# Sums of squares and first-part scaling in the last part of a hybrid attention trunk, rearranged over VectorE, TensorE and GpSimd

## The chip, the cores and the metric

The kernel runs on one core of one Trainium2 chip, in float32 (products are split into a rounded high part and a low part, three matmuls for each). The metric is the device time of one execution in microseconds, given as the median of several runs.

## The reference

One layer of a decoder trunk over 1,024 tokens of width 2,048: two groups of attention heads, an output projection, a gated embedding, and a last normalisation. What the change touches is the end:

```python
gate = jax.nn.sigmoid(rmsnorm(h, norm_ple_g[i]) @ w_ple_gate[i])
h = h + gate * (p[i] @ w_ple_proj[i])
return rmsnorm(h, norm_final_g)

def rmsnorm(x, g, eps=NORM_EPS):
    xf = x.astype(jnp.float32)
    y = xf * lax.rsqrt(jnp.mean(xf * xf, axis=-1, keepdims=True) + eps)
    return (y * g.astype(jnp.float32)).astype(x.dtype)
```

The last `rmsnorm` needs, for each token, the sum of squares over all 2,048 features before any feature of that token can be scaled and written.

## The kernel before

Features lie on the partitions: the 2,048 are 16 chunks of 128, and tokens run along the free axis. The 1,024 tokens are two halves of 512. The last stage finishes the second of them to be done, half 0. Chunks u and u + 8 are worked as a pair u = 0 to 7, held in `hpair[u]`, [128, 2, 512], with c = 0 or 1 for the member of the pair. For each pair TensorE makes two gate products, called S3 and A22, into one PSUM bank; VectorE adds and multiplies, ScalarE applies the sigmoid, VectorE adds gate times embedding to h, and the squares of h are added up in the tile `s2`.

Pairs 0 to 5 run in a loop over the whole half. Pairs 6 and 7 are written out by hand, in two quarters of 256 tokens: `TQ[0]` (the first part) and `TQ[1]` (the last quarter). The steps, each for a pair u, a member c and a quarter tq:

- `partly(u, nm, tq)`: the 24 matmuls (8 chunks, three each, L2055 to L2057) of one gate product on one quarter; it can call a function between its two halves of 12.
- `begun`: two VectorE operations, L2062 (adds the PSUM bank) and L2063 (times the root that the gate's normalisation needs).
- `sigm`: sigmoid on ScalarE, L2067.
- `ended`: two VectorE operations, L2072 (times the embedding, in PSUM) and L2073 (adds to h).
- `squared`: the square on ScalarE, L2081; for the very last one, pair 7, c = 0, last quarter, on VectorE, L2079.
- `gained`: ScalarE multiplies h by the last normalisation's weight, L2086.
- `mean`: matmuls with a constant matrix of 1/128 sum `s2` and the four squares of pairs 6 and 7 over the partitions, for the first part (L2091, L2093). `root` makes the inverse root from it (L97 to L101).
- `finals(u)`: VectorE multiplies pair u of the first part by the root, [128, 2, 256], L1955, and SyncE issues its transfer to the output, L1956.
- `mean_t`: the sums for the last quarter, with tokens on the partitions: each matmul takes 128 tokens of squares as weights and one column of the constant (L2100, L2102); `j` is which 128 tokens. `root_t` makes the root (L2116 to L2121).
- `turned`: TensorE transposes the last quarter's blocks (L2134) so that `leave` can multiply by the root, one value for each partition, on ScalarE (L2143) or VectorE (L2145) and send them (L2148, L2151): eight blocks of 256 KB.
- `late.popleft()()`: products of the other half that wait to be written, L1963 on VectorE.

TensorE, VectorE and ScalarE execute this in the order written. GpSimd's and SyncE's instructions are put in order by a planner that plays the program through with its own costs; each queue then executes in that fixed order, so a transfer that waits for its data holds what is queued behind it.

## Time and profile before

| | before |
|---|---|
| median of 3 runs | 2390.8 us (2389.43 to 2391.39) |
| profiled execution, its own time | 2393.36 us |
| its span | 2391.5 us |
| TensorE matmul busy | 2360.9 us (99%) |
| VectorE busy | 1864.1 us (78%) |
| ScalarE busy | 1201.7 us (50%) |
| GpSimd busy | 238.6 us (10%) |
| granted TensorE clock, mean | 0.998 |

The profile is of one execution; times in it are microseconds from the start of its span. PE is TensorE, DVE VectorE, ACT ScalarE, POOL GpSimd, SPq the queue from which SyncE issues transfers. A timeline row has the start, the duration, the engine, the line, what is written and read, and how many instructions were merged into it; a bracket tells how long the engine had been idle and what released it. Rows of matmuls overlap, so their pace is the distance between starts. A row of the view by windows has the stretch, its length, the busy time of PE, PE weight loads, DVE, ACT and POOL with their counts, then the granted clock, the DMA engines' share and GB/s.

### The profile page before, as it was taken

What the parts mean: (1) busy time and instruction counts of PE and PEld (TensorE: products, weight loads), DVE (VectorE), ACT (ScalarE), POOL (GpSimd) and SP (SyncE); (2) the same over time, 40 slices, a digit from 0 to 9 for tenths busy, and PEclk for the clock granted to TensorE, in tenths of its full rate; (3) what the DMA queues carried; (4) which work ended last, traced back from release to release, by engine and by line L of the source; (5) the groups of instructions that cost most, each with busy time, mean ns of one, the idle gap of its engine ahead of it and who ended that gap; (6) DMA issues with size and microseconds to landing.
All of it is one profiled execution on the core that took longest, in us unless ns stands there. A gap on an engine that the chain in (4) does not pass through costs nothing.

```text
span 2391.5 us, 32647 instructions
## 1 busy us (share of the span) xinstructions
PE 2360.9 (99%) x11318; PEld 1969.1 (82%) x11318; DVE 1864.1 (78%) x3245; ACT 1201.7 (50%) x2163; POOL 238.6 (10%) x367
## 2 busy tenths in 40 slices
PE   9999999999999999999999999999999999999998
PEld 7787878888888888888888888888788888778877
DVE  7888777777877778788888876766887987677787
ACT  6243345555556445555555556545642435532455
POOL 1211110000000000000000000110121121011000
PEclk9999999999999999999999999999999999999999
DMA  8787765444456777434444455666798889898965
GB/s 266 264 284 231 233 209 156 149 156 135 125 148 215 257 251 255 127 107 114 117 122 126 112 158 187 202 200 214 215 234 192 267 245 278 291 342 294 320 206 183
DMA packets 219413, 489.53 MB, mean 205 GB/s; under 512 B 24688, under 2 KB 36208, under 8 KB 219248
## 3 DMA queue, kind: packets, MB, share of 16 engines
q1 hardware_dynamic: 159728, 347.43, 44.3%
q0 software_dynamic: 42960, 109.86, 18.0%
q10 hardware_dynamic: 16560, 30.15, 3.7%
q8 instruction: 89, 1.46, 0.2%
q14 instruction: 76, 0.62, 0.1%
HBM read 336.09 MB, written 159.65 MB: 207 GB/s over the span
## 4 chain that ended last, share of the span: by engine, by line
PE 80%; issue 7%; DMA 5%; DVE 4%; ACT 3%; POOL 1%; SPq 0%; ACTq 0%; POOLq 0%; DVEq 0%
PE acc L240 14%; PE acc L242 14%; PE acc L241 14%; PE tp L415 2%; PE pbc L630 2%; PE pbc L628 2%; PE pbc L629 2%; PE z L319 1%; PE z L318 1%; PE pa L630 1%; PE pa L628 1%; PE pb L1733 1%; PE pb L1734 1%; PE pb L1735 1%; PE pa L629 1%
## 5 line engine op out<-in xcount | busy, mean ns | idle before, releaser
L240 PE MATMUL acc<-xh,whi 128*128 128x512 f32 x1152 | 464.6, 403 | 0.0
L242 PE MATMUL acc<-xh,wlo 128*128 128x512 f32 x1152 | 450.8, 391 | 0.1
L241 PE MATMUL acc<-xl,whi 128*128 128x512 f32 x1152 | 450.3, 391 | 0.0
L162 ACT CAST whi<-wraw 128x1024 fp32r<-128x1024 f32 x192 | 201.7, 1050 | 123.4 <-PE acc L241 109.5
L242 PEld LDWEIGHTS acc<-xh,wlo 128*128 128x128 f32 x1152 | 216.2, 188 | 48.2 <-DVE wlo L157 0.5
L721 ACT CAST wpr<-T 128x512 fp32r<-128x512 f32 x144 | 87.8, 620 | 325.3 <-DVE T L680 228.4
L241 PEld LDWEIGHTS acc<-xl,whi 128*128 128x128 f32 x1152 | 217.2, 189 | 37.7 <-issue 0.2
L240 PEld LDWEIGHTS acc<-xh,whi 128*128 128x128 f32 x1152 | 216.8, 188 | 38.1 <-issue 0.2
L157 DVE TENSOR_TENSOR wlo<-wraw,whi 128x1024 fp32r<-128x1024 f32 x160 | 195.4, 1221 | 45.2 <-ACT whi L162 43.2
L434 ACT CAST awh<-tp 128x256 fp32r<-128x256 f32 (+1 forms) x160 | 80.6, 504 | 167.4 <-PE tp L415 166.8
L370 ACT ACTIVATE et<-z,mx 128x512 f32<-128x512 f32 (+7 forms) x128 | 94.7, 740 | 61.7 <-DVE mx L364 53.3
L439 DVE TENSOR_TENSOR awl<-tp,awh 128x256 fp32r<-128x256 f32 (+1 forms) x160 | 92.4, 578 | 41.7 <-ACT awh L434 41.5
L721 ACT CAST wpr<-wraw 128x512 fp32r<-128x512 f32 x112 | 68.6, 615 | 105.3 <-DMA wraw<-tw_d 38.1
L349 DVE TENSOR_TENSOR_SCAN st<-pt 128x511 f32<-128x511 f32 (+3 forms) x64 | 86.7, 1355 | 22.3 <-ACT pt L342 20.7
L735 DVE TENSOR_TENSOR wpr<-T,wpr 128x512 fp32r<-128x512 f32 x144 | 98.6, 685 | 3.6 <-ACT wpr L721 2.3
L364 DVE TENSOR_REDUCE mx<-z 128x1 f32<-128x512 f32 (+7 forms) x128 | 97.0, 758 | 4.4
L735 DVE TENSOR_TENSOR wpr<-wraw,wpr 128x512 fp32r<-128x512 f32 x112 | 76.0, 685 | 20.2 <-ACT wpr L721 20.2
L240 PE MATMUL acc<-cA12h,whi 128*128 128x512 f32 x192 | 75.9, 395 | 0.0
L240 PE MATMUL acc<-cA11h,whi 128*128 128x512 f32 x192 | 75.6, 394 | 0.0
L342 ACT ACTIVATE pt<-z 128x512 f32<-128x512 f32 (+3 forms) x64 | 41.6, 650 | 67.0 <-DVE z L326 63.1
L241 PE MATMUL acc<-cA12l,whi 128*128 128x512 f32 x192 | 75.2, 392 | 0.0
L242 PE MATMUL acc<-cA12h,wlo 128*128 128x512 f32 x192 | 75.1, 391 | 0.0
(580 smaller groups left out, 6206.9 us busy)
## 6 DMA issues: line engine op xcount, KB each, us to landing
wraw<-w_in SPq DMA_DIRECT2D x192, 512.0 KB, 3.7
wraw<-w_gate SPq DMA_DIRECT2D x92, 256.0 KB, 5.9
wraw<-w_out SPq DMA_DIRECT2D x72, 256.0 KB, 4.5
wraw<-w_vg SPq DMA_DIRECT2D x71, 256.0 KB, 4.3
wlo_d<-wlo SPq DMA_DIRECT2D x32, 512.0 KB, 3.6
wlo<-wlo_d SPq DMA_DIRECT2D x32, 512.0 KB, 4.3
h_d<-hc POOLq DMA_DIRECT2D x56, 256.0 KB, 4.9
comb_d<-sg POOLq DMA_DIRECT2D x48, 256.0 KB, 7.4
```

What stands on the lines that cost most here:

```text
L157: V.tensor_tensor(lo[:, o], raw[:, o], hi[:, o].bitcast(F32), op=ALU.subtract)
L162: side.later(1, lambda: A.copy(hi[:, o], raw[:, o]))
L240: T.matmul(acc[c], hi[:, k2, kh, c, :], xh, start=first, stop=False)
L241: T.matmul(acc[c], hi[:, k2, kh, c, :], xl, start=False, stop=False)
L242: T.matmul(acc[c], lo[:, k2, kh, c, :], xh, start=False, stop=last)
L349: V.tensor_tensor_scan(st[:, off + 1:nkey], pt[:, off:nkey - 1], pt[:, off:nkey - 1], initial=1.0, op0=ALU.mult, op1=ALU.bypass)
L364: V.reduce_max(mx, z[:, vw], axis=AX.X, negate=True)
L370: A.activation(et[:, vw], z[:, vw], AF.Exp, bias=mx[:, 0:1], accum_out=l)
L434: A.copy(wh[:, o, :], tp[:, o, :])
L439: V.tensor_tensor(wl[:, o, :], tp[:, o, :], wh[:, o, :].bitcast(F32), op=ALU.subtract)
L721: A.copy(t[:, 0], src)
L735: V.tensor_tensor(t[:, 1], src, t[:, 0].bitcast(F32), op=ALU.subtract)
```

## The change

For the first part, the squares of three of the four blocks of pairs 6 and 7 are added into `s2` by VectorE (`fold`), so that `mean` has two matmuls where it had five; and `mean` is called between the two halves of the second S3 product of the last quarter, where it stood ahead of that product. For the last quarter, the sums of pairs 6 and 7 (c = 1), which stood in the middle of the last gate product, are made behind it, after the first transposes, in one PSUM tile of two columns where there were two tiles; `root_t` handles the two columns in one operation. The transposes into `ps` stand behind the last sums. Pairs 2 to 5 of the first part are multiplied by GpSimd (`eng=G`), and pairs 6 and 7 by VectorE at earlier places.

```diff
-        def final(r, u):
+        def final(r, u, eng=V):
             t = hpair[u][:, :, TQ[0]]
-            V.tensor_tensor(t, t, r.unsqueeze(1).to_broadcast([P, 2, Q]), op=ALU.mult)
+            eng.tensor_tensor(t, t, r.unsqueeze(1).to_broadcast([P, 2, Q]), op=ALU.mult)
...
-        def mean(*es):
+        def fold(u, c):
+
+            V.tensor_tensor(s2[:, TQ[0]], s2[:, TQ[0]], sqs.pop((u, c, 0)), op=ALU.add)
+
+        def mean():
 
             ms[0] = pp.tile([P, Q], F32, name="ssps", tag="t")
             T.matmul(ms[0], ones, s2[:, TQ[0]], start=True, stop=False)
-            for e in es:
-                T.matmul(ms[0], ones, sqs.pop(e + (0,)), start=False, stop=e == (7, 0))
+            T.matmul(ms[0], ones, sqs.pop((7, 0, 0)), start=False, stop=True)
 
         def mean_t(*es):
 
+            new = 1 not in ms
+            if new:
+                ms[1] = pp.tile([P, 2], F32, name="ssps", tag="t")
             for j in range(2):
-                if (1, j) not in ms:
-                    ms[1, j] = pp.tile([P, 1], F32, name="ssps", tag="t")
-                    T.matmul(ms[1, j], s2[:, Q + j * P:Q + j * P + P], ones[:, 0:1], start=True, stop=False)
+                o, js = ms[1][:, j:j + 1], slice(j * P, j * P + P)
+                if new:
+                    T.matmul(o, s2[:, TQ[1]][:, js], ones[:, 0:1], start=j == 0, stop=False, skip_group_check=True)
                 for e in es:
-                    T.matmul(ms[1, j], sqs[e + (1,)][:, j * P:j * P + P], ones[:, 0:1], start=False, stop=e == (7, 0))
+                    T.matmul(o, sqs[e + (1,)][:, js], ones[:, 0:1], start=False, stop=e == (7, 0) and j == 1, skip_group_check=True)
...
         def root_t():
-            for j in range(2):
-                A.activation(rq[:, j:j + 1], ms[1, j], AF.Ln, bias=eps6[:, 0:1], scale=1.0 / NK)
+            A.activation(rq, ms[1], AF.Ln, bias=eps6[:, 0:1], scale=1.0 / NK)
             A.activation(rq, rq, AF.Exp, scale=-0.5)
-            for j in range(2):
-                V.scalar_tensor_tensor(rn[:, j:j + 1], ms[1, j], EPS * NK, rq[:, j:j + 1], op0=ALU.add, op1=ALU.mult)
+            V.scalar_tensor_tensor(rn, ms[1], EPS * NK, rq, op0=ALU.add, op1=ALU.mult)
...
         begun(6, 0, 0)
+        fold(6, 1)
         squared(7, 1, 0)
...
         begun(7, 0, 0)
+        fold(7, 1)
         squared(6, 0, 0)
...
         tables(LOGS)
+        fold(6, 0)
         late.popleft()()
         begun(6, 1, 1)
-        mean((6, 1), (7, 1), (6, 0), (7, 0))
-        partly(7, "S3", 1)
+        partly(7, "S3", 1, mean)
         root()
         tables(SIGS)
         finals(0)
+        finals(2, 3, 4, 5, eng=G)
         begun(7, 1, 1)
...
-        partly(7, "A22", 1, lambda: mean_t((6, 1), (7, 1)))
-        finals(2, 3, 4)
+        partly(7, "A22", 1)
         ended(6, 0, 1)
...
-        finals(5)
+        finals(6)
         zA = pz.tile([P, 2, HALF], F32, name="oz", tag="z")
         ps = [pp.tile([P, HALF], F32, name="oa", tag="acc", bufs=2) for _ in range(2)]
         for j in range(2):
             turned(zA[:, j, :], 0, j)
-        turned(ps[0], 1, 0)
-        mean_t((6, 0))
-        turned(ps[1], 1, 1)
+        mean_t((6, 1), (7, 1), (6, 0))
         ended(7, 0, 1)
         squared(7, 0, 1)
         gained(7, 0, 1)
-        finals(6)
+        finals(7)
         mean_t((7, 0))
+        for j in range(2):
+            turned(ps[j], 1, j)
...
         leave(zA[:, 1, :], 0, 1, A)
-        finals(7)
         leave(zB[:, 0, :], 2, 0, A)
```

More of the change, by code (lines that the diff above doesn't have):

```diff
@@ L2114, in root_t, with finals @@
         def root_t():
-            for j in range(2):
-                A.activation(rq[:, j:j + 1], ms[1, j], AF.Ln, bias=eps6[:, 0:1], scale=1.0 / NK)
+            A.activation(rq, ms[1], AF.Ln, bias=eps6[:, 0:1], scale=1.0 / NK)
             A.activation(rq, rq, AF.Exp, scale=-0.5)
-            for j in range(2):
-                V.scalar_tensor_tensor(rn[:, j:j + 1], ms[1, j], EPS * NK, rq[:, j:j + 1], op0=ALU.add, op1=ALU.mult)
+            V.scalar_tensor_tensor(rn, ms[1], EPS * NK, rq, op0=ALU.add, op1=ALU.mult)
             V.scalar_tensor_tensor(rn, rn, -0.5 / NK, rq, op0=ALU.mult, op1=ALU.mult)
             V.scalar_tensor_tensor(rq, rn, 1.5, rq, op0=ALU.add, op1=ALU.mult)
-        def finals(*us):
+        def finals(*us, eng=V):
             for u in us:
-                final(r0, u)
+                final(r0, u, eng)
         BLOCKS = [[(u, 0) for u in range(4)], [(u, 1) for u in range(4)],
```

## The prediction

> **What bounds the kernel now.** I read the page first, then the timelines of TensorE, VectorE, ScalarE and SyncE over the last 40 us, then the busy time by windows of the last ten.

> ```profile
> span 2391.5 us, 32647 instructions
> PE 80%; issue 7%; DMA 5%; DVE 4%; ACT 3%; POOL 1%; SPq 0%; ACTq 0%; POOLq 0%; DVEq 0%
> ```

> The chain that ended last is TensorE for 80% of the span, so until the last product of the last quarter every TensorE instruction taken out is worth its pace. The change touches only what is issued after about 2354 us. These are TensorE's rows there that matter (start, duration; duration overlaps, so the pace is read from the starts):

> ```profile
> 2364.65 0.59 PE L2091 MATMUL ssps<-s,onesr 128*128 128x256 f32 x2
> 2365.08 1.89 PE L2093 MATMUL ssps<-sq,onesr 128*128 128x256 f32 x8
> 2366.62 0.47 PE L2055 MATMUL pbq<-cgS3h,wpr 128*128 128x256 f32 x1
> 2366.93 0.28 PE L2056 MATMUL pbq<-cgS3l,wpr 128*128 128x256 f32 x1
> 2367.05 0.28 PE L2057 MATMUL pbq<-cgS3h,wpr 128*128 128x256 f32 x1
> ...
> 2374.00 0.28 PE L2100 MATMUL ssps<-onesr,s 128*128 128x1 f32 x2
> ...
> 2375.26 0.36 PE L2055 MATMUL pbq<-cgA22h,wpr 128*128 128x256 f32 x1
> 2375.46 0.28 PE L2056 MATMUL pbq<-cgA22l,wpr 128*128 128x256 f32 x1
> ...
> 2376.77 1.04 PE L2134 MATMUL oz<-ident,h 128*128 128x128 f32 x8
> ...
> 2379.77 0.61 PE L2102 MATMUL ssps<-onesr,sq 128*128 128x1 f32 x4 [0.68 <-DVE sq L2079]
> ```

> TensorE runs without a gap to the last product, which ends at 2376.77. From there VectorE, ScalarE and the transfers set the end: TensorE itself then waits 0.68 us for the last square. VectorE's rows:

> ```profile
> 2360.97 0.42 DVE L2072 TENSOR_TENSOR qt<-qt,ple 128x256 f32<-128x256 f32 x1 [0.48 <-ACT qt L2067]
> ...
> 2363.80 0.42 DVE L2072 TENSOR_TENSOR qt<-qt,ple 128x256 f32<-128x256 f32 x1 [0.48 <-ACT qt L2067]
> ...
> 2367.97 0.42 DVE L99 SCALAR_TENSOR_TENSOR r<-ssps,r 128x256 f32<-128x256 f32 x1 [1.83 <-ACT r L98]
> ...
> 2369.34 0.69 DVE L1955 TENSOR_TENSOR h<-h,r 128x512 f32<-128x512 f32 x1
> 2369.95 0.42 DVE L2062 TENSOR_TENSOR qt<-pbq,qt 128x256 f32<-128x256 f32 x1
> 2370.41 0.42 DVE L2063 TENSOR_TENSOR qt<-qt,sums 128x256 f32<-128x256 f32 x1
> ...
> 2373.39 0.42 DVE L2063 TENSOR_TENSOR qt<-qt,sums 128x256 f32<-128x256 f32 x1
> 2373.73 1.89 DVE L1955 TENSOR_TENSOR h<-h,r 128x512 f32<-128x512 f32 x3
> 2375.53 0.41 DVE L2072 TENSOR_TENSOR qt<-qt,ple 128x256 f32<-128x256 f32 x1
> ...
> 2376.97 0.42 DVE L2062 TENSOR_TENSOR qt<-pbq,qt 128x256 f32<-128x256 f32 x1 [0.56 <-PE pbq L2057]
> 2377.43 0.43 DVE L2063 TENSOR_TENSOR qt<-qt,sums 128x256 f32<-128x256 f32 x1
> 2377.78 0.68 DVE L1955 TENSOR_TENSOR h<-h,r 128x512 f32<-128x512 f32 x1
> 2378.38 0.41 DVE L2072 TENSOR_TENSOR qt<-qt,ple 128x256 f32<-128x256 f32 x1
> ...
> 2379.29 0.42 DVE L2079 TENSOR_TENSOR sq<-h 128x256 f32<-128x256 f32 x1
> ...
> 2381.39 0.16 DVE L2121 SCALAR_TENSOR_TENSOR r<-r,r 128x2 f32<-128x2 f32 x1
> ```

> Here VectorE has no gap from 2367.97 to 2376.4, so it is nearly as full as TensorE. The root of the last quarter is ready at 2381.55, and only then can the eight output blocks leave. How they leave:

> ```profile
> 2382.30 1.31 SPq L2148 DMA_DIRECT2D out_dram<-hc  x3
> 2383.71 0.41 SPq L1956 DMA_DIRECT2D out_dram<-h  x1
> 2384.21 0.62 SPq L2151 DMA_DIRECT2D out_dram<-hc  x1
> ```
> ```profile
> 2384.00:2385.00 1.00, 0.00 (x0) 0.00 (x0) 0.00 (x0) 1.00 (x3) 0.00 (x0) 1.00 1.05 385
> 2388.00:2389.00 1.00, 0.00 (x0) 0.00 (x0) 0.00 (x0) 0.00 (x0) 0.00 (x0) 0.50 1.04 342
> ```

> The two columns at the end are the DMA share and GB/s: all 16 engines are full, at about 345 GB/s, to the end. Eight blocks of the last quarter and one of the first part (the row at L1956 that stands between them) drain here, 9 x 262,144 B, some 6.8 us.

> **The change, part by part.** *Sums of the first part.* Five products of squares become two. The five run from 2364.65 to 2366.62: 1.97 us, 0.394 each. Three fewer take 1.18 us from TensorE; the two that stay still switch between the two kinds of product once, as now (the 0.31 from 2366.62 to 2366.93 in place of the pace of 0.12 from 2366.93 to 2367.05). They also move behind twelve products, 12 x 0.12 = 1.44 us, so the sum itself comes 1.44 - 1.18 = 0.26 us later, and with it VectorE's steps from 2367.97 on.

> *The three folds* are VectorE operations of 128x256, 0.42 us each. The first two fall where VectorE now waits 0.48 us for a sigmoid, the third in the 1.83 us before L99: nothing. The cover is thin for the first two; what ran over would come out of the same 1.83 us. TensorE's new wait, for the third fold, is at about 2366.1, and the fold ends by about 2365.1; queued behind it are twelve products, so a late fold would cost TensorE directly, but it has 1 us in hand.

> *The last quarter's sums* leave the middle of the last product: 2374.00 to 2375.26, 1.26 us, and the slower restart (0.20 to 2375.46 in place of 0.12), 1.34 us in all. The last product then ends at 2376.77 - 1.18 - 1.34 = 2374.25, and VectorE's 0.56 us of waiting for it at 2376.97 goes. The moved sums stand where TensorE waits for the last square anyway.

> *Four blocks to GpSimd.* VectorE loses three in the row at 2373.73 (to 2375.53, 1.80 us) and one at 2377.78 (to 2378.38, 0.60 us); one that came after the square, block 6, now lies before it (0.60). What is late next is ScalarE: with nothing between, a sigmoid separates L2063 from L2072 by 0.91 us (0.43 running, 0.48 waiting as in the row at 2360.97). So the last stretch is, from the L2063 of block (6,0), now at 2373.39: +0.26 for the late root, +0.91 to its L2072 at 2374.56, +0.46 and +0.35 (the pitches from 2376.97 to 2377.43 and 2377.78, which the pair L2072, L2073 shares) to the next L2062 at 2375.37, the same to block 6 at 2376.18, +0.60 to the last L2072 at 2376.78, +0.91 to the square (2378.38 to 2379.29 now) at 2377.69. That is 1.60 us before 2379.29.

> *The root of the last quarter* does two operations on ScalarE and VectorE as one each:

> ```profile
> 2378.33 1.28 ACT L2105 ACT_TABLE_LOAD   x1
> 2379.62 0.51 ACT L2086 ACTIVATE qt<-h,gvec 128x256 f32<-128x256 f32 x1
> 2380.19 0.48 ACT L2116 ACTIVATE r<-ssps,eps 128x1 f32<-128x1 f32 x2
> ```

> Half of 0.48 is 0.24, and VectorE's pair gives 0.07 more. The root is then ready 1.60 + 0.31 = 1.91 us earlier, at 2379.6. The table load and the gain hang on the last sigmoid, which moves by the same 1.60, so they end as closely before the sums as now.

> *The leaving blocks.* They start 1.91 us earlier. Block 7 of the first part, now fourth in this queue, is finished by 2378.7 and has drained before the first block leaves: one of nine transfers, 262,144 B at 345 GB/s, 0.76 us (0.50 if SyncE's issue sets the pace: 2383.71 to 2384.21). I take 0.66. The transposes that move behind the last sums are done by the time their copies ask for them.

> The sum is -1.91 - 0.66 = **-2.6 us**: a span of 2388.9, and a run of 2393.36 - 2.6 = 2390.8 for the profiled one. That run lay 2.56 above the median of the runs shown, 2390.8; against the median the forecast is **2388.2**.

> **What GpSimd's operations cost.** No arithmetic of GpSimd is in the trace. The nearest rows:

> ```profile
> 973.20 0.96 POOL L1394 MEMSET qz<- 128x1024 f32 x1 [9.04 <-PE tp L415]
> ```
> ```profile
> 973.77 0.69 DVE L1427 TENSOR_TENSOR qk<-qk,sw 128x512 f32<-128x512 f32 x1
> ```

> GpSimd writes 1,024 elements in 0.96 us, 512 in 0.48: one pass over a block. A product reads two and writes one, so it costs 0.48 to 1.44 us; I take 1.2, near three passes. Four of them, from 2369.6, end at 2374.4, behind them SyncE issues their transfers in its own order, then blocks 1, 6, 7. The leaving blocks come at 2380.4 (2382.30 less 1.91); up to 2369.6 + 4p + 4 x 0.76 = 2380.4, p = 1.9 us each, the four are covered, and at 2.6 each (4 x 0.65 = 2.6 us later) their transfers would have eaten up the gain. [...]

> A second unknown is what it does to VectorE. In these rows a VectorE product of two SBUF tensors takes its usual 0.69 us while the memset runs, so the lower bound is nothing, and I take nothing. The upper bound is that they take turns, the first rival.

> **The rivals.** *Turns.* If a GpSimd product and a VectorE operation with two SBUF operands exclude each other, GpSimd gets in whenever VectorE runs L2062 or L2072, whose one operand is in PSUM. It then holds the next operation, L2063 or L2073, for 1.2 less the 0.46 between them (2369.95 to 2370.41): 0.74 us, four times, 3.0 us. All of it lands on the chain above, which is VectorE's: -2.6 + 3.0 = +0.4, 2391.2 (2390.4 at 1.0 us a product, 2392.1 at 1.44). For it: VectorE is full from 2369 on, and seven of its operations there have two SBUF operands. Against it: the memset's row, which reads nothing and so tests only half. [...]

> *Turns with a long product.* If GpSimd's first products are slower than three passes, as code it has not run before here, the same mechanism ends on the other side. At (2.6 + 4.8) / 4 + 0.46 = 2.3 us each the kernel is 4.8 us (0.2%) slower; at 2.5 us it is 8.2 - 2.6 = +5.6, 2396.4. Against it: 2.3 us would be nearly five passes.

> *More gain.* With VectorE never in the way, the last square still needs the last product at 2374.25 and the chain behind it: from 2376.77 to 2379.29 now, less the 0.60 of L1955 in it, 1.9 us. That is at most 1.5 us better than forecast, 2386.7, still within 0.2%.

> **How the numbers follow.** Side by side 0.52, turns 0.36, turns with a long product 0.12. About 0.2%, 4.8 us, is what a measurement of this kernel can tell from no change. The first two lie within it; I give 0.06 of the first to faster, for runs that scatter (2389.43 to 2391.39 before) and terms read too small, and 0.11 of the last to slower. So 0.06, 0.83, 0.11. The range goes from the most gain, 2386.7, less 0.7 of scatter, 2386.0, to turns at 1.44 us a product, 2392.1, with 1.4 of scatter, 2393.5; it leaves the long product out.

> **What would show it.** Right: two products of squares in the middle of the second S3 product and L2055 to L2057 without a gap otherwise; the last product ending near 2374.3; four GpSimd rows of about 1.2 us; VectorE's L2063 and L2073 beside them at 0.42; the last square about 1.6 us earlier; no L1956 transfer among the leaving blocks. Turns would show as L2063, L2073 or L1955 rows lengthened to over 1 us, or gaps before them, each ending with a GpSimd row. Wrong altogether: GpSimd rows over 2 us, SyncE holding finished blocks behind them, or a TensorE gap before the moved sums.

## The result: 0.15% slower, and the profile after

The median went from 2390.7 us (15 runs, 2388.09 to 2393.65) to 2395.6 us (15 runs, 2391.28 to 2398.08): a ratio of 1.0015, 95% interval 1.0008 to 1.0022, or 1.9 to 5.3 us slower. The forecast was 2388.2, with 2386.0 to 2393.5 as its range; the measured median lies above it.

The profiled execution after the change has a span of 2390.8 us (2392.68 us its own time), less than the 2391.5 before. That isn't the change: whole executions scatter by some us ahead of the part that it touches. So everything below is read in the *tail*: from the end of pair 6's S3 product on the last quarter (with the change, the start of pair 7's) to the end of the span. Before, that is 2364.65 to 2391.5, 26.85 us; with the change, 2361.20 to 2390.8, **29.60 us**, 2.75 longer. A later profile of each gave 26.86 and 29.66, with starts at 2361.94 and 2364.64: the tail repeats to 0.1 us, its start doesn't repeat to 3.

VectorE's timeline with the change, from the first part's root on (columns as before):

```profile
2366.65 0.42 DVE L2062 TENSOR_TENSOR qt<-pbq,qt 128x256 f32<-128x256 f32 x1
2367.10 1.06 DVE L2063 TENSOR_TENSOR qt<-qt,sums 128x256 f32<-128x256 f32 x1
2368.08 1.78 DVE L1955 TENSOR_TENSOR h<-h,r 128x512 f32<-128x512 f32 x1
2369.79 0.41 DVE L2072 TENSOR_TENSOR qt<-qt,ple 128x256 f32<-128x256 f32 x1
2370.23 1.07 DVE L2073 TENSOR_TENSOR h<-h,qt 128x256 f32<-128x256 f32 x1
2371.22 0.41 DVE L2072 TENSOR_TENSOR qt<-qt,ple 128x256 f32<-128x256 f32 x1
2371.66 1.04 DVE L2073 TENSOR_TENSOR h<-h,qt 128x256 f32<-128x256 f32 x1
...
2377.08 0.42 DVE L2079 TENSOR_TENSOR sq<-h 128x256 f32<-128x256 f32 x1
...
2380.69 0.16 DVE L2125 SCALAR_TENSOR_TENSOR r<-r,r 128x2 f32<-128x2 f32 x1
```

L2063 and L2073 took 0.42 or 0.43 before, L1955 0.69. Four of them are longer here by 0.64, 1.09, 0.64 and 0.62: 2.99 us. L2062 and L2072, which take one operand from PSUM, are as before. There is no gap: the waiting is inside the row, counted as busy. GpSimd's timeline, one row at a time:

```profile
2366.24 1.64 POOL L1955 TENSOR_TENSOR h<-h,r 128x512 f32<-128x512 f32 x1 [89.96 <-DVE r L101]
```
```profile
2367.84 1.47 POOL L1955 TENSOR_TENSOR h<-h,r 128x512 f32<-128x512 f32 x1
```
```profile
2369.27 1.74 POOL L1955 TENSOR_TENSOR h<-h,r 128x512 f32<-128x512 f32 x1
```

Each lengthened VectorE row ends 0.3 us (L1955 0.6 us) after one of these: VectorE's operation seems to begin when GpSimd's is over. The fourth starts at 2370.97 and takes 1.45. Now TensorE:

```profile
2362.64 0.59 PE L2095 MATMUL ssps<-s,onesr 128*128 128x256 f32 x2
2363.07 0.59 PE L2096 MATMUL ssps<-sq,onesr 128*128 128x256 f32 x2
2363.32 0.47 PE L2055 MATMUL pbq<-cgS,wpr 128*128 128x256 f32 x1
...
2370.58 0.28 PE L2057 MATMUL pbq<-cgA22h,wpr 128*128 128x256 f32 x1
2374.50 1.18 PE L2138 MATMUL oz<-ident,h 128*128 128x128 f32 x8 [3.64 <-issue]
2375.48 0.42 PE L2106 MATMUL ssps<-onesr,s 128*128 128x1 f32 x2
...
2377.47 2.27 PE L2108 MATMUL ssps<-onesr,sq 128*128 128x1 f32 x10
2379.60 1.95 PE L2138 MATMUL oa<-ident,h 128*128 128x128 f32 x8
2381.34 1.92 PE L2138 MATMUL oz<-ident,h 128*128 128x128 f32 x8
```

The last product is early, as forecast. Then TensorE stands for 3.64 us. The bracket names no releaser; in the kernel's text the first transposes reuse the PSUM space that block (6,0) reads last in its L2072, and that L2072, late on VectorE, ends at 2374.40, 0.1 us before they start. The transposes from 2379.60 then go at 0.22 us each (1.74 us for eight); before, eight took 0.93 us (2380.23 to 2381.16). The view by windows shows why; the third column from the end is the granted clock:

```profile
2374.50:2375.00 0.50, 0.50 (x5) 0.50 (x6) 0.50 (x2) 0.11 (x1) 0.00 (x0) 1.00 0.00 0
2375.00:2375.50 0.50, 0.50 (x7) 0.50 (x5) 0.47 (x2) 0.50 (x2) 0.00 (x0) 0.81 0.00 0
2375.50:2376.00 0.50, 0.50 (x5) 0.50 (x4) 0.50 (x2) 0.50 (x2) 0.00 (x0) 0.50 0.00 0
...
2385.50:2386.00 0.50, 0.00 (x0) 0.00 (x0) 0.00 (x0) 0.21 (x1) 0.00 (x0) 0.95 1.04 348
```

Less than a microsecond after TensorE has taken up work again, its clock falls to one half, and it stays there for 10.2 us, to the end of its work. Before, it fell at 2385.5, 3.2 us after the last transpose, where it cost nothing. The last quarter's sums, which were to be done as the last square comes, are now late:

```profile
2379.78 0.26 ACT L2121 ACTIVATE r<-ssps,eps 128x2 f32<-128x2 f32 x1 [1.85 <-PE ssps L2108]
```

and the blocks leave with a hole, since the fourth waits for transposes (ScalarE's copy for it starts at 2383.29, after a wait of 1.14 us for them): SyncE's timeline has no block of the first part among them, as forecast, but the fourth issue starts 1.1 us after the third has ended.

```profile
2381.60 1.31 SPq L2152 DMA_DIRECT2D out_dram<-hc  x3
2384.00 0.62 SPq L2155 DMA_DIRECT2D out_dram<-hc  x1
```

### The profile page after: what moved, and what is told of

It is laid out like the page before. It is cut to its first block, busy times and chain, and to the rows that moved or that the text cites. A ratio compares the mean times of both kernels' runs of the same rounds, so it can differ in the third digit from the quotient of the medians.

```text
span 2390.8 us, 32644 instructions
## 1 busy us (share of the span) xinstructions
PE 2361.9 (99%) x11312; PEld 1971.8 (82%) x11312; DVE 1865.2 (78%) x3243; ACT 1202.2 (50%) x2162; POOL 244.9 (10%) x371
## 4 chain that ended last, share of the span: by engine, by line
PE 75%; issue 11%; DVE 5%; DMA 4%; ACT 3%; POOL 2%; ACTq 0%; POOLq 0%; SPq 0%; DVEq 0%
PE acc L240 14%; PE acc L242 14%; PE acc L241 14%; PE tp L415 2%; PE pbc L630 2%; PE pbc L628 2%; PE pbc L629 2%; PE z L319 1%; PE z L318 1%; PE av L462 1%; DMA wraw<-w_gate 1%; PE av L461 1%; PE av L460 1%; PE pb L1733 1%; PE pb L1734 1%
```

## The experiments

Every kernel's tail, cut at the end of the last square (L2079) and at the last step of the last quarter's root, in us, all from the profiled executions:

| kernel | tail starts | to last square | to root | to the end | tail |
|---|---|---|---|---|---|
| before | 2364.65 | 15.06 | 1.84 | 9.95 | 26.85 |
| before, again | 2361.94 | 15.05 | 1.85 | 9.96 | 26.86 |
| the change | 2361.20 | 16.30 | 3.35 | 9.95 | 29.60 |
| the change, again | 2364.64 | 16.32 | 3.37 | 9.97 | 29.66 |
| before + GpSimd | 2367.36 | 17.24 | 2.53 | 9.97 | 29.74 |
| change without GpSimd | 2359.53 | 15.16 | 2.27 | 9.94 | 27.37 |
| change, TensorE kept busy | 2363.23 | 16.35 | 1.78 | 9.34 | 27.47 |
| without GpSimd, kept busy | 2359.66 | 15.14 | 1.79 | 9.61 | 26.54 |
| the same, pair 6 moved | 2361.72 | 14.55 | 2.03 | 9.10 | 25.68 |
| before + first part's sums | 2363.34 | 14.54 | 1.85 | 9.97 | 26.36 |
| before + last quarter's sums | 2366.68 | 14.40 | 1.95 | 9.97 | 26.32 |
| best of these parts | 2361.91 | 14.55 | 1.79 | 9.15 | 25.49 |

Theory at this point: GpSimd and VectorE take turns (3.0 us), and the pause that this leaves on TensorE halves its clock (some 2.5 us). Rival: one of the two is only a by-product.

**GpSimd alone.** On the kernel before:

```diff
         finals(0)
+        finals(2, 3, 4, 5, eng=G)
...
-        finals(2, 3, 4)
...
-        finals(5)
```

> The kernel before, with one part of the change alone: pairs 2 to 5 of the first part are multiplied by GpSimd, all else as before. The tail is counted from the first matmul of pair 7's S3 product on the last quarter (for the kernels before: from the end of pair 6's) to the end of the span: 26.85 us before (from 2364.65), 29.60 with the whole change (from 2361.20). Theory (turns, and a TensorE left idle by them): GpSimd's four take 1.45 to 1.75 us each, VectorE's L2063, L1955 and L2073 beside them lose about 3.0 us, which is paid for by the 1.8 and 0.6 us of products that VectorE no longer makes and the 0.56 us in which it waited for TensorE; TensorE has the last quarter's sums in the middle of its last product and is not idle for 3 us, so its clock stays at 1.0. Tail 26.4 to 27.4, time within 0.5 us of before. Rival A (GpSimd's products alone make the change slow): tail 29 or more, 2 to 3 us slower. Rival B (no turns): tail 26.2.

Measured: tail 29.74, ratio of the runs 1.0015 (1.0006 to 1.0024). Rival A's size: this part alone costs all that the whole change costs, 2.89 us. The theory's turns were there (L2063 1.07, L1955 1.78, L2073 1.06 and 1.04), but what I had paid for them with was wrong: here the squares of ScalarE behind those L2073 are needed in the middle of TensorE's last product. TensorE's timeline:

```profile
2377.82 0.38 PE L2102 MATMUL ssps<-onesr,sq 128*128 128x1 f32 x2 [0.83 <-ACT sq L2081]
2379.23 0.38 PE L2102 MATMUL ssps<-onesr,sq 128*128 128x1 f32 x2 [1.03 <-ACT sq L2081]
```

With these two waits, 1.86 us, the sums in the middle took 3.44 us (2376.70 to 2380.14) where they took 1.26, and the product's end went from 12.12 to 14.3 us after the tail's start. The clock, which the theory had at 1.0, fell here too, from 2381.7 to 2385.1, though no single pause was over 1.03 us.

**The change without GpSimd.** On the changed kernel:

```diff
-        finals(2, 3, 4, 5, eng=G)
...
         partly(7, "A22", 1)
+        finals(2, 3, 4)
...
+        finals(5)
         finals(6)
```

> The whole change, but pairs 2 to 5 stay on VectorE, 2, 3 and 4 ahead of the L2072 of block (6,0) and 5 ahead of pair 6. Theory: VectorE is held by nobody; TensorE ends its last product 2.5 us earlier than before and then waits about 1.6 us for block (6,0), too short for its clock to fall; last square as before or 0.1 later, root 0.2 earlier, one transfer fewer among the leaving blocks: tail about 26.0 (0.85 less than before), time 2389.5 to 2390.5 where before has 2390.7. Rival (moving the sums behind the last product is what costs, with or without GpSimd): TensorE's clock falls here too and the tail is 28 or more.

Measured: tail 27.37, ratio 1.0001 (0.9992 to 1.001). The square is where the theory had it (0.1 later), but the clock fell, at 2372.4, after a pause of 1.89 us:

```profile
2371.07 1.07 PE L2138 MATMUL oz<-ident,h 128*128 128x128 f32 x8 [1.89 <-issue]
...
2373.57 2.27 PE L2108 MATMUL ssps<-onesr,sq 128*128 128x1 f32 x10
```

Both were wrong on the size: 27.37 lies between 26.0 and 28. "Too short for its clock to fall" was a guess, and it fell. So the rest of the change loses time without GpSimd too, but less than the rival said.

**TensorE kept busy.** On the changed kernel:

```diff
         partly(7, "A22", 1)
+        warm = pp.tile([P, Q], F32, name="warm2", tag="t")
+        for _ in range(24):
+            T.matmul(warm, W[7, "A22", 1][0][:, 0:P], op.XC["gA22", 4][0][:, TQ[1]], start=True, stop=True)
```

> The whole change, with 24 further matmuls of 128x256 behind the last product (into a bank that nobody reads), 2.9 us, so that TensorE isn't idle before the transposes. Theory (the idle 3.64 us let the granted clock fall to 0.5, and sums and transposes ran at half pace): the clock stays at 1.0 until the end, the sums are made as the last square comes, the root is ready 1.8 us earlier and the blocks leave without gaps: tail about 27.0, 2.6 us less than with the change, VectorE's lengthened rows unchanged. Rival (the clock is a by-product, the turns alone set the tail): tail 29.6 as with the change, or more by what the further matmuls hold up.

Measured: tail 27.47, ratio 1.0006 (0.9997 to 1.0015). Useless work takes 2.13 us off the tail, with VectorE's lengthened rows as they were: the clock is a cause of its own. It held until the sums were made (square to root 1.78 in place of 3.35) and fell at 2380.8, so that the later transposes were slow again. Of the 0.47 missing to 27.0, 0.28 is the root (1.52 us earlier where 1.8 was forecast) and the rest lies in the leaving blocks:

```profile
2376.57 1.06 PE L2138 MATMUL oz<-ident,h 128*128 128x128 f32 x8 [0.82 <-PE warm L2216]
...
2381.22 1.91 PE L2138 MATMUL oz<-ident,h 128*128 128x128 f32 x8
```

**The operations by themselves.** A kernel of its own:

```python
for i in range(4):
    gop(i)                      # GpSimd: the product of L1955, 128x512
for i in range(12):             # the four forms, one after the other
    V.tensor_tensor(va[:, 0:Q], vb[:, 0:Q], vc[:, 0:Q], op=ALU.mult)
...
V.tensor_copy(x[:, 0:2], va[:, 0:2])   # behind n VectorE operations
for k in range(64):
    T.matmul(z[0], w, x[:, 0:Q], start=True, stop=True)
```

> None of the reference is computed: the disputed operations by themselves. First GpSimd's product of 128x512 four times alone, then beside VectorE products of two SBUF tensors, of one PSUM and one SBUF tensor, of one SBUF tensor and a scalar, and beside ScalarE. Then bursts of 64 matmuls after pauses of 2 to 14 VectorE operations. Theory: 1.1 to 1.2 us each alone and beside the PSUM form and ScalarE, 1.4 to 1.8 beside the form with two SBUF tensors, whose rows grow from 0.42 to about 1 us; TensorE's granted clock falls only after pauses of over 3 us, and not after 2 us or less. Rival: GpSimd's product takes 1.5 us even alone, so the rows of VectorE are lengthened by something else; or the clock falls after any pause.

GpSimd's timeline; the stages are alone, two SBUF tensors, one PSUM and one SBUF tensor, one SBUF tensor and a scalar:

```profile
10.25 4.98 POOL L46 TENSOR_TENSOR h<-h,r 128x512 f32<-128x512 f32 x4 [9.80 <-DVE r L52]
16.19 5.59 POOL L46 TENSOR_TENSOR h<-h,r 128x512 f32<-128x512 f32 x4 [0.97 <-DVE r L52]
27.02 4.93 POOL L46 TENSOR_TENSOR h<-h,r 128x512 f32<-128x512 f32 x4 [5.24 <-DVE r L52]
34.19 5.07 POOL L46 TENSOR_TENSOR h<-h,r 128x512 f32<-128x512 f32 x4 [2.25 <-DVE va L75]
```

VectorE's timeline beside them; the last row is VectorE without GpSimd, eight products with both operands in SBUF:

```profile
15.96 9.32 DVE L63 TENSOR_TENSOR va<-vb,vc 128x256 f32<-128x256 f32 x12
...
26.79 5.41 DVE L69 TENSOR_TENSOR va<-ps,vc 128x256 f32<-128x256 f32 x12
...
33.96 8.17 DVE L75 TENSOR_SCALAR va<-vb,vc 128x256 f32<-128x256 f32 x12
...
49.55 3.58 DVE L86 TENSOR_TENSOR va<-vb,vc 128x256 f32<-128x256 f32 x8
```

A product costs GpSimd 1.24 us alone (4.98 / 4; 4.94 / 4 beside ScalarE), close to the 1.2 that I took. Twelve VectorE products with an operand in PSUM take 5.41 us, the pace that VectorE has without GpSimd (3.58 for eight), and slow nobody; with both in SBUF they take 9.32, 3.9 us more, 1.0 for each of GpSimd's four, and GpSimd loses 0.6 in all. The longest single VectorE row was 1.42 us. The form with one SBUF tensor and a scalar is held too: 8.17 us for twelve, with rows of 0.23 to 1.37. So a second SBUF tensor is not needed for it; of the forms tried, the one that reads PSUM went free. This is the theory's side: turns, by operation, at VectorE's cost.

TensorE's timeline, bursts of 64 matmuls, which take 7.93 us at full clock; the bracket is the pause ahead:

```profile
66.69 7.93 PE L100 MATMUL z<-x,w 128*128 128x256 f32 x64 [2.29 <-DVE x L98]
77.83 9.42 PE L100 MATMUL z<-x,w 128*128 128x256 f32 x64 [3.21 <-DVE x L98]
...
134.09 7.93 PE L100 MATMUL z<-x,w 128*128 128x256 f32 x64 [1.37 <-DVE x L98]
144.31 9.41 PE L100 MATMUL z<-x,w 128*128 128x256 f32 x64 [2.29 <-DVE x L98]
```

After pauses of 1.37 us (three of them) no burst lost time; after 2.29 us three of four lost 1.5 us; after 3.21 us or more all did. In the burst at 77.83 the clock fell at 79.4, 1.6 us after work had begun, and rose at 82.8. So my 3 us as the least pause was too long, and the fall came after the pause here (ahead of the burst at 91.38 it came inside the pause, at 89.7).

**Without GpSimd and kept busy.** On the kernel without GpSimd, `keep(n)` being n matmuls into a bank that is not read:

```diff
         partly(7, "A22", 1)
+        keep(14)
...
         mean_t((6, 1), (7, 1), (6, 0))
+        keep(6)
```

> The change without GpSimd, as in the run before of that kind (tail 27.37), with 14 further matmuls behind the last product and 6 behind the first group of the last quarter's sums, into a bank that nobody reads, so that TensorE doesn't pause for 1.9 us. Theory (what that run lost of its forecast, 26.0, went to the clock alone, which fell 3 us after the pause): clock 1.0 until the last transposes, sums as the last square comes, root 0.7 us earlier, blocks leaving without gaps, tail 25.9 to 26.3. Rival (the transposes behind the last sums are late by their place in the order, clock or not): tail 27 or more.

Measured: tail 26.54, ratio 0.9998 (0.9988 to 1.0007). Better by 0.83 than without the further matmuls, but 0.2 to 0.6 short: the clock held through the sums and fell at 2375.7, in the middle of the transposes (eight in 1.59 and 1.92 us). With the kernels above this makes a square of tails, one profile each (the further matmuls are 24 in one place with GpSimd, 14 and 6 without): with GpSimd 29.60 and, kept busy, 27.47; without it 27.37 and 26.54. GpSimd costs 2.23, or 0.93 where TensorE is kept busy; the pause costs 2.13, or 0.83 without GpSimd. They meet: each makes the other dearer.

**Pair 6 behind the last square.** On that kernel:

```diff
         finals(5)
-        finals(6)
...
-        finals(7)
+        finals(6, 7)
```

> The same, with pair 6's product moved from before the last L2072 to behind the last square. Theory: VectorE is the bound there, so the square comes 0.6 us earlier; pairs 6 and 7 fill the time in which VectorE waits for the root, which then comes 0.4 to 0.6 earlier: tail 25.3 to 25.7, about 1.3 us less than before the change (26.85), time about 2389.5 where before has 2390.9; too little for the runs to tell. Rival (transfers set the end, whatever the root does): tail as in the run without this move.

Measured: tail 25.68, ratio 0.9994 (0.9985 to 1.0003). The tail is where the theory had it, at the upper end, and the square came 0.59 earlier; but the root came 0.35 earlier, not 0.4 to 0.6, and 0.51 comes from the leaving blocks. The clock this time stayed at 1.0 to the last transpose, without anything in the edit aiming at that, so that part of the agreement is luck:

```profile
2377.04 1.07 PE L2138 MATMUL oa<-ident,h 128*128 128x128 f32 x8
2377.95 1.04 PE L2138 MATMUL oz<-ident,h 128*128 128x128 f32 x8
```

**The first part's sums alone**, on the kernel before (`fold` and `mean` as in the change):

```diff
-        mean((6, 1), (7, 1), (6, 0), (7, 0))
-        partly(7, "S3", 1)
+        partly(7, "S3", 1, mean)
```

> The kernel before with the first part's sums alone as the change has them: three folds on VectorE, two matmuls of squares between the halves of the second S3 product. Theory: TensorE gains 1.18 us there, but then waits 0.8 us for the squares that the sums in the middle of its last product need; VectorE's L99 comes 0.14 later, the last square 0.4 earlier; no clock fall: tail 26.3 to 26.6 (before 26.85). Rival (a full gain of 1.18 us): tail 25.7.

Measured: tail 26.36, 0.49 less, as the theory had it; TensorE waits 0.41 us in one place for a square (0.8 forecast), the last square comes 0.52 earlier (0.4 forecast), and the clock stays at 1.0 while TensorE has work.

**The last quarter's sums alone**, on the kernel before (`mean_t` and `root_t` as in the change):

```diff
-        partly(7, "A22", 1, lambda: mean_t((6, 1), (7, 1)))
+        partly(7, "A22", 1)
...
-        turned(ps[0], 1, 0)
-        mean_t((6, 0))
-        turned(ps[1], 1, 1)
+        mean_t((6, 1), (7, 1), (6, 0))
...
         mean_t((7, 0))
+        for j in range(2):
+            turned(ps[j], 1, j)
```

> The kernel before with the last quarter's sums alone as the change has them: behind the last product, in one bank, the root's operations on both columns at once, and the transposes into the two further banks behind the last sums. Theory: TensorE ends its last product 1.34 us earlier and finds its first transposes free at once (no pause over 1 us, so the clock stays at 1.0), VectorE no longer waits 0.56 us, the root is 0.87 us earlier: tail 25.9 to 26.3. Rival (thin work, one-column products and transposes, lets the clock fall without a pause): clock 0.5 before the last sums, tail 27 or more.

Measured: tail 26.32, 0.53 less, at the theory's edge; the root came 0.55 earlier (0.87 forecast). The clock fell at 2381.4, as the last sums were made, though no pause was over 0.45 us, so the rival had a point:

```profile
2378.08 1.07 PE L2135 MATMUL oz<-ident,h 128*128 128x128 f32 x8 [0.45 <-PE pbq L2057]
...
2381.77 1.95 PE L2135 MATMUL oa<-ident,h 128*128 128x128 f32 x8
```

Both parts that aren't GpSimd's gain 0.5 us each by themselves.

**The best of these parts.** On the kernel with the first part's sums: one bank and one root as in the change, the sums left in the middle of the product, and

```diff
-        finals(6)
+        finals(6, 7)
...
-        finals(7)
```

> The kernel before with the first part's sums as the change has them, the last quarter's sums where they were, in one bank with the root's operations on both columns at once, and pair 7's product moved ahead of the root beside pair 6's. No GpSimd, no further matmuls. Theory (VectorE's chain and the clock set the tail; sums in the middle of a product keep TensorE busy): clock 1.0 to the end, root 0.2 to 0.3 us earlier than with the first part's sums alone (16.39 after the tail's start), eight blocks leaving in 9.1 to 9.3: tail 25.2 to 25.6, time 1.2 to 1.6 us under before, at the edge of what the runs tell. Rival (pair 7's product delays the root by the 0.6 us that it takes): tail 26 or more.

Measured: tail 25.49, 1.36 less than before and within the theory's range, though not by its steps: against the first part's sums alone the root came 0.05 earlier, not 0.2 to 0.3, and 0.82 comes from the leaving blocks (9.97 to 9.15), among which pair 7 no longer is. The clock stays at 1.0 while TensorE has work, and the two products end as the root's step is due:

```profile
2376.38 1.28 DVE L1955 TENSOR_TENSOR h<-h,r 128x512 f32<-128x512 f32 x2
2377.69 0.16 DVE L2123 SCALAR_TENSOR_TENSOR r<-ssps,r 128x2 f32<-128x2 f32 x1
```

The runs give 0.9993 (0.9984 to 1.0002), median 2389.38 against 2391.42: the interval still holds 1, so that it beats the kernel before is shown in the tail and not in the time. It beats the changed kernel's 1.0015 by both.

**Both kernels again.**

> The kernel before once more, for its profile alone: how far the tail repeats. Theory (the tail is set by VectorE's chain and the clock, the scatter of whole runs comes from what lies ahead of it): tail 26.7 to 27.0 (26.85 before), its start 1 to 4 us from 2364.65. Rival (the tail scatters as whole runs do): off by more than 0.5 us.

> The whole change once more, for its profile alone. Theory: VectorE's lengthened rows repeat to 0.1 us and the clock falls again within 4.5 us of TensorE's last product; the tail is 29.6, or less by up to 1 us where the clock rises again before the last transposes. Rival: no fall of the clock this time, tail about 27.5.

Measured: tails 26.86 and 29.66; starts 2.7 us earlier and 3.4 us later than in the first profiles. The lengthened rows were 1.07, 1.78, 1.06 and 1.05, the pause 3.66 us, the clock 0.5 from 2378.7. Both theories held.

## Why the prediction was wrong

Its steps, in the tail's terms (us against before):

| step | forecast | measured |
|---|---|---|
| first part's root | +0.26 | +0.14 |
| end of the last product | -2.52 | -2.6 |
| VectorE beside GpSimd | 0 | +2.99 |
| last square | -1.60 | +1.24 |
| last square to root | -0.31 | +1.51 |
| blocks leaving | -0.66 | 0.00 |
| tail | -2.6 | +2.75 |

**Right:** the three matmuls of squares saved, the folds in VectorE's gaps, the last product 2.5 us earlier, 1.2 us for one of GpSimd's products (1.24 alone, 1.45 to 1.74 in turns with VectorE), no block of the first part among the leaving ones.

**The first step that failed** is "the lower bound is nothing, and I take nothing" for what GpSimd does to VectorE. I took it from a memset that ran beside a VectorE product, and a memset reads nothing. The rival *turns* had the mechanism, and its term, 4 x 0.74 = 3.0 us, was measured at 2.99; the sum agrees better than its parts, which were 0.62 to 0.64 three times and 1.09 once. The rows it named were the ones, but for an L1955 in place of one L2063. With this term the forecast of the last square becomes -1.60 - 0.12 (the root's +0.14 in place of +0.26) + 2.99 = +1.27, against +1.24 measured. The rows that started beside GpSimd show it: with two SBUF operands they took 1.04 to 1.07 us in place of 0.42 or 0.43, and 1.78 in place of 0.69; with one operand in PSUM they took 0.41 or 0.42, as before. I had put this rival behind a memset's row that couldn't test it. The form with a scalar, which the kernel doesn't have beside GpSimd, waited as well in the run by itself (rows of up to 1.37 us).

**The second** is the sentence that the moved sums "stand where TensorE waits for the last square anyway", and the one on the transposes that are "done by the time their copies ask for them". Both take TensorE's pace as given. Neither the forecast nor a rival asked what the clock does when TensorE has nothing to do; a gap ahead of the moved sums stands among the signs of being wrong, but without a price. Moving work off the end of a full TensorE made a pause: 3.64 us with the turns, 1.89 without GpSimd. At half clock the ten sums take 4.12 us (2375.48 to 2379.60), 0.41 each in place of 0.21 (1.26 / 6 before), and square to root grows by 1.51 where 0.31 was to be saved; the slow transposes open the hole among the leaving blocks that eats the 0.66. So *turns* too was wrong by its sum: +0.4 forecast, +2.75 measured, the difference all behind the last square. Whether the forecast would have come true side by side isn't shown: without GpSimd the tail is 27.37, not 24.3, but there VectorE makes the four products itself, 2.4 us at 0.60 each.

The clock's side of it, as the runs show it: the nine changes read in the run of the operations by themselves lie on one grid of 3.413 us, and the clock stayed low for 3.4 us in the burst at 77.83, one stretch of that grid, and for 10.2 us, three stretches, with the change.

**What remains open.** The medians of the two kernels differ by 4.9 us, the tails by 2.75 to 2.80. The interval of the ratio holds the tail's figure; whether anything else differs ahead of the tail, whose start scattered from 2359.5 to 2367.4 over all these kernels, the runs don't tell. Each tail is one profile, two for before and the change, and where the clock's grid lies differs between executions (the fall came 20.82 and 21.10 us after the tail's start in the two profiles of before). The two profiles of the change met it alike (the fall came 14.11 and 14.10 us after the tail's start), so how much of the 2.75 us another execution loses is not shown; nor is it for the other tails in which the clock fell. A GpSimd share timed so that it meets only VectorE operations with an operand in PSUM was not tried.

## What to carry to other kernels

Before work goes to GpSimd, list the VectorE operations that will run beside it and have no operand in PSUM (both forms tried without one were held): each of GpSimd's products held one of them for 0.6 to 1.1 us, and the trace shows it as a longer busy row, not as a gap. Before work is taken off a full TensorE, ask whether what follows keeps it full: a pause of 1.89 us near the end was followed by 6.8 us at half clock here (the change without GpSimd), and of the four of 2.29 us in the run of the operations by themselves three cost 1.5 us each, by where they lay on the clock's grid. Where whole runs scatter more than the change can bring, compare the stretch behind a fixed instruction; here it repeated to 0.1 us.

## What the runs showed of the hardware that I had not expected

The clock fell while TensorE was at work: 0.8 us after it resumed with the change, 1.6 us into a burst. It fell without a pause worth the name (0.45 us at most, with the last quarter's sums alone), and it stayed low although TensorE's rows were back to back (from 2375.31 to 2384.96 with the change).

The grid accounts for these cases if the one-column sums are left out. Take the stretches of 3.413 us counted from a change of the clock, in the ten of these twelve profiles in which one was read (not that of the first part's sums alone, nor that with pair 6 moved), and add up the time of the products and transposes alone. At full clock it fell after every stretch with 44% or less (24% with the change, 26% with the last quarter's sums alone, 23% with TensorE kept busy, 32% without GpSimd, 40% with that kept busy, 44% with GpSimd alone) and after none with 45% or more (45% with the best of these parts). With the change it then stayed low after stretches with 5% and 74% and rose after one with 83%. With the sums counted in, no such order comes out: stretches 89 to 97% busy ended in a fall, while others 71 to 80% busy did not. That the sums hardly count is read from these ten profiles; no run tests it by itself.

So with a change of order that left TensorE's work as it was (pair 6 behind the last square) the clock stayed up, at 1.00 in every window from 2371 to 2380, where 40% came just before the fall without it. Where its own stretches lie was not read. Whether another execution, with the grid elsewhere, would keep it up is not shown.
